# A transformer layer on one core: the last output projection but one asked for earlier, weight sums one group later, later loads tied

## The chip, the cores and the metric

One NeuronCore of a Trainium2 chip runs the whole program. The metric is the device time of one execution in microseconds (us), as a median of several runs. Engines are named as in the profile: PE (TensorE matmuls; PEld is its weight loads), DVE (VectorE), ACT (ScalarE), POOL (GpSimd), SP (SyncE, which here only issues DMAs).

## The reference, cut to what matters

One layer, 2048 tokens, width 1024, feed-forward width 4096, all float32:

```
h = rmsnorm(x, norm_mix) * (1 + sc_a) + sh_a
x = x + g_a * hybrid_mixer(h, ...)           # stick-breaking attention and gated delta rule, then @ w_out
h = rmsnorm(x, norm_mlp) * (1 + sc_m) + sh_m
x = x + g_m * (square(relu(h @ w_ff1)) @ w_ff2)
```

The change concerns the end of the mixer (`@ w_out`), the second norm and the feed-forward.

## The kernel before

**Precision.** A float32 product is made of three float32r matmuls: every operand is split into a rounded part and a rest (`hm`/`lm`, `who`/`wlo`, `bh`/`bl`, `swh`/`swl`), ACT makes the rounded part by a cast and DVE or POOL the rest by a subtraction.

**Mixer.** The tokens are four chunks of 512, worked from chunk 3 down to chunk 0. `project_out(c)` (L943 to L968) multiplies a chunk's mixed heads by `w_out`: it loads 8 tiles `mx`, splits them into `hm` and `lm` (L950, L132), makes 8 output tiles of 24 matmuls each (192 in all, L221 to L223), adds the residual (L959), stores the sum to `x1_d[c]`, and collects its squares. `outs(c)` calls it and asks for the norm's factors. Chunk 0's delta rule is a chain that goes from engine to engine in small steps (L901 to L939); a branch (L575) stands inside it, whose body is not entered here.

**Feed-forward.** It runs in two halves of 1024 tokens, `hf` 1 (chunks 2, 3) and then `hf` 0. Both products use a scheme of 7 block products in place of 8, which needs sums of blocks. The right sides of the first product, `bs` (28 split tiles), are made from `x1_d`: each tile is loaded, scaled twice (`load_x`, L1095), summed on POOL and split (`split_right`). For `hf` 1 that is written out at L1117 to L1129, for `hf` 0 in `load_h` (L1195 to L1227). `ff1` (L1249) runs 16 groups `g` of 7 products with 12 matmuls each (84 a group, L1260 to L1262); its left sides come from `lefts1` (four loads `A` of 256 KB, four POOL sums `s`, split by `left`, L1139). Its result goes to `h_d` in seven parts. `ff2` (L1307) runs 112 products of 12 matmuls (L1337 to L1339), each with a weight `w` and a right tile `bl` loaded and split; its sums `y` start from `x1_d` (`load_y`, L1228).

**The weight sums.** `w_ff2` has to be summed as well. `sums2(g)` (L1237) does it during `hf` 1: it loads 1 MB into two tiles `ws`, makes two sums on POOL (L1242, L1244) and two on DVE (L1243, L1245), and stores 1 MB to `w2_d[g]`. It is called ahead of `ff1(hf, g, ...)`.

**What sets the order.** A scheduler builds each engine's list of instructions before the run: it goes by the order of the program, with `tc.high_priority()` pulling work ahead and `tc.issue_after(x)` keeping an instruction behind `x`. On the chip every engine takes its list strictly in turn, so an instruction that waits holds up all behind it.

Of the kernel before, what the change touches and what calls it, by code (L numbers as in the profile page):

```python
# [7 lines left out]
F32 = mybir.dt.float32  # L8
# [49 lines left out]
def tile_hybrid_layer(  # L58
# [17 lines left out]
    nc = tc.nc  # L76
# [57 lines left out]
    if True:  # L134
# [17 lines left out]
        def full(tag, name, bufs=1, dt=F32, pool=None):  # L152
            return (pool or np_).tile([P, CH], dt, tag=tag, name=name, bufs=bufs)
# [46 lines left out]
        late = []  # L200

        def run_late():

            todo, late[:] = late[:], []
            for f in todo:
                f()
# [849 lines left out]
        def outs(*which):  # L1056
            for o_ in which:
                acc = project_out(o_)
                if o_:
                    out_rstd(o_, acc)  # L1060
                accs2[o_] = acc
# [33 lines left out]
        def load_x(hf, rs, x, k, i, n):  # L1095
            kk = k + 4 * i
            nc.sync.dma_start(x, x1_d[2 * hf + n][:, kk, :])
            V.tensor_tensor(x, x, rs[n], ALU.mult)
            A.activation(x, x, AF.Identity, scale=g2[:, kk:kk + 1], bias=mods[:, 24 + kk:25 + kk])
            return x  # L1100
# [5 lines left out]
        outs(2)  # L1106
        run_late()
        run_late()
        rs1 = [full("acc1", "frs2"), full("wab", "frs3", pool=k1)]
        for n in range(2):  # L1110
            nc.sync.dma_start(rs1[n], rs_d[2 + n])
# [4 lines left out]
        for k in range(4):  # L1116
# [10 lines left out]
            split_right(bs[5][k], x22)  # L1127
            G.tensor_tensor(x21, x22, x21, SUB)
            split_right(bs[3][k], x21)  # L1129
        outs(1, 0)  # L1130

        casts = []

        def left(x, name, eng):  # L1139

            wh = wp.tile([P, CH], F32R, tag="wh", name="swh" + name)
            wl = wp.tile([P, CH], F32R, tag="wl", name="swl" + name)
            with tc.high_priority():
                casts.append(A.copy(wh, x).ins)  # L1144
                eng.tensor_tensor(wl, x, wh.bitcast(F32), SUB)  # L1145
            return wh, wl

        def lefts1(hf, g, unit):

            nm = f"{hf}_{g}"  # L1150
            a = []
            with tc.high_priority():
                for i, t in enumerate(AB):
                    u = unit(t, f"{t}_1{nm}")
                    gate["w1"] = nc.sync.dma_start(u, w_ff1[g, i]).ins
                    a.append(u)
                a11, a12, a21, a22 = a
                s4, s5, s2, s6 = [unit("S", f"s{i}{nm}") for i in (4, 5, 2, 6)]
                G.tensor_tensor(s4, a21, a22, ADD)
                G.tensor_tensor(s5, s4, a11, SUB)  # L1160
                G.tensor_tensor(s2, a12, s5, SUB)
                G.tensor_tensor(s6, a11, a21, SUB)
            xs = (a11, a12, s2, a22, s4, s5, s6)
            return lambda j: left(xs[j], f"{nm}_{j}", V)

# [29 lines left out]
        def load_h(hf, rs):  # L1195
            bs = rights(hf)

            def load(tag, i, n):
                return [load_x(hf, rs, unit(tag, f"fx{hf}{k}{i}{n}"), k, i, n) for k in range(4)]

            def split(j, xs):
                for k in range(4):
                    split_right(bs[j][k], xs[k])

            def sub(o, x, y):
                for k in range(4):
                    G.tensor_tensor(o[k], x[k], y[k], SUB)

            x11, x12 = load("A11", 0, 0), load("A12", 0, 1)
            split(0, x11)  # L1210
            sub(x11, x12, x11)
            split(4, x11)
            x22 = load("A22", 1, 1)
            sub(x11, x22, x11)
            split(5, x11)
            split(2, x22)
            sub(x12, x22, x12)
            split(6, x12)
            x21 = load("A21", 1, 0)
            sub(x11, x11, x21)  # L1220
            split(3, x11)
            split(1, x21)
            return bs
# [11 lines left out]
        def sums2(g):  # L1235

            y = [fy.tile([P, N2], F32, tag="y", name=f"ws2_{g}_{i}") for i in range(3)]  # L1237
            (a11, a12), (a21, a22), (s4, s5) = [(t[:, 0:CH], t[:, CH:N2]) for t in y]
            for i in range(2):
                with tc.issue_after(gate["w1"]):  # L1240
                    nc.sync.dma_start(y[i].rearrange("p (i c) -> p i c", i=2), w_ff2[g, 2 * i:2 * i + 2].rearrange("i p c -> p i c"))
            G.tensor_tensor(s4, a21, a22, ADD)  # L1242
            V.tensor_tensor(s5, s4, a11, SUB)  # L1243
            G.tensor_tensor(a11, a11, a21, SUB)  # L1244
            V.tensor_tensor(a12, a12, s5, SUB)  # L1245
            for i in range(2):
                nc.sync.dma_start(w2_d[g][:, 2 * i:2 * i + 2], y[2 - 2 * i].rearrange("p (i c) -> p i c", i=2))

        def ff1(hf, g, bs, get):  # L1249
            nm = f"{hf}_{g}"  # L1250
# [56 lines left out]
        def ff2(hf, q, ys, base):  # L1307


            n1, n2 = 0, CH  # L1310
            dst = {0: ((0, n1),), 1: ((0, n1),), 5: ((0, n2),), 2: ((0, n2),), 4: ((4, n2),), 6: ((4, n1), (4, n2)),
                   3: ((4, n1),)}
            chain = {0: "u", 5: "u", 6: "u", 4: "v", 2: "v", 3: "p", 1: "q"}
            a, banks = q % 2, {}
            side = {"u": a, "v": 1 - a, "p": 1 - a, "q": a}
            final = {n: j for j in ORDER for n in dst[j]}
            for n, j in enumerate(ORDER):
                ch = chain[j]
                start = ch not in banks
                if start:  # L1320
                    banks[ch] = [pf.tile([P, CH], F32, tag=f"f{side[ch]}", name=f"f2{hf}_{q}_{j}{m}") for m in range(4)]
                for i in range(8):
                    g = 8 * q + i
                    nm = f"2{hf}_{g}_{j}"
                    x, bt = unit("S", "w" + nm), right_tile(nm)
                    nc.sync.dma_start(x, {0: w_ff2[g, 0], 1: w_ff2[g, 1], 3: w_ff2[g, 3]}[j] if j in (0, 1, 3) else
                                      w2_d[g][:, {4: 0, 5: 1, 6: 2, 2: 3}[j], :])
                    nc.sync.dma_start(bt[1].bitcast(F32), h_d[hf][g][:, j, :])
                    at = 56 * q + 8 * n + i
                    with tc.issue_after(casts[base + max(at - 22, at // 4 - 3)]):  # L1330
                        A.copy(bt[0], bt[1].bitcast(F32))  # L1331
                    V.tensor_tensor(bt[1], bt[1].bitcast(F32), bt[0].bitcast(F32), SUB)  # L1332
                    wh, wl = left(x, nm, G)
                    for m in range(4):
                        s = slice(m * P, (m + 1) * P)
                        ps = banks[ch][m]
                        T.matmul(ps, lhsT=wh[:, s], rhs=bt[0], start=start and i == 0, stop=False, skip_group_check=True)  # L1337
                        T.matmul(ps, lhsT=wh[:, s], rhs=bt[1], start=False, stop=False, skip_group_check=True)  # L1338
                        T.matmul(ps, lhsT=wl[:, s], rhs=bt[0], start=False, stop=i == 7, skip_group_check=True)  # L1339
                with tc.high_priority():  # L1340
                    for m in range(4):
                        for m0, cs in dst[j]:
                            y = ys[m0 + m][:, cs:cs + CH]
                            gt = ngate[:, m0 + m:m0 + m + 1] if j == 3 else mods[:, 40 + m0 + m:41 + m0 + m]
                            V.scalar_tensor_tensor(y, banks[ch][m], gt, y, ALU.mult, ALU.add)  # L1345
                            if q == 1 and final[m0, cs] == j:
                                nc.sync.dma_start(yTv[:, m0 + m, hf * N2 + cs:hf * N2 + cs + CH], y)
# [3 lines left out]
        def get(j):  # L1351
            return first.get(j) or rest(j)

        for hf in (1, 0):
            if not hf:
                get = lefts1(0, 0, unit)
            for g in range(NG):
                more = lefts1(hf, g + 1, unit) if g + 1 < NG else None
                if hf:
                    sums2(g)  # L1360
                ff1(hf, g, bs, get)
                get = more
                if hf and g == 1:
                    for f in rstd([accs2[0]], "2", "20", pf, "f0"):
                        f()
                if not hf and g == 4:
                    ys = load_y(0)
            if hf:
                ys = load_y(1)
            base = len(casts)  # L1370
            for q in range(2):
                ff2(hf, q, ys, base)
            if hf:
                bs = load_h(0, [accs2[0], accs2[1]])
# [88 lines left out]
```

## Time and profile before

| | us |
|---|---|
| median of 3 runs (lowest, highest) | 2860.49 (2858.39, 2870.82) |
| the profiled execution | 2859.91 |
| its span, first to last instruction | 2858.1 |
| PE busy in the span | 2579.9 |
| DVE, ACT, POOL busy | 1651.4, 1286.4, 1041.4 |

PE has the most busy time, so PE's idle time and the time that it spends at its lower clock are what a change can win back. The profile's column PEclk gives the granted clock as a share of the full 2.4 GHz; half of it is 1.2 GHz. Stages are best read one by one, since each has another limit.

### The profile page before, as it was taken

To read this page: it belongs to the slowest core of one execution; us is meant where nothing else is said; L and a number is where in the kernel's file an instruction comes from. 1 tells how busy PE (TensorE), PEld (TensorE's weight loads), DVE (VectorE), ACT (ScalarE), POOL (GpSimd) and SP (SyncE) were. 2 spreads that over 40 slices of the span, in tenths; PEclk is the share of its full clock that TensorE was granted. 3 is DMA by queue.
4 is the path that set the end of the run, shared out by engine and by line. 5 is a ranking of instruction groups with operands and counts; after the bars stand their busy time and mean duration, and the time that the engine had idled before them with its cause. 6 is when DMAs were issued, how large, how long until landed. Compare 5 with 4: busy or idle time off the path is not lost. (4 is left out here: it accounts for less than half of the span.)

```text
span 2858.1 us, 40676 instructions
## 1 busy us (share of the span) xinstructions
PE 2579.9 (90%) x13684; PEld 2105.0 (74%) x13684; DVE 1651.4 (58%) x3359; ACT 1286.4 (45%) x2622; POOL 1041.4 (36%) x837
## 2 busy tenths in 40 slices
PE   4998789899999999899288988889999999999999
PEld 2787568877787787777167777767887888878887
DVE  7653886377445774257554655576556544476551
ACT  4552453245334454245343444455443555564441
POOL 3222200040012201021235666654447555655444
PEclk9999889999999999899599999999999999999999
DMA  9786687574556556453265666696664464476664
GB/s 305 271 293 209 201 281 255 161 226 156 175 172 199 186 172 208 132 170 117 64 191 193 214 210 214 217 364 217 194 192 148 138 212 151 155 263 197 194 186 130
DMA packets 327314, 566.85 MB, mean 198 GB/s; under 512 B 33512, under 2 KB 80552, under 8 KB 327080
## 3 DMA queue, kind: packets, MB, share of 16 engines
q1 hardware_dynamic: 308904, 534.63, 57.2%
q10 hardware_dynamic: 18176, 29.37, 2.8%
q8 instruction: 114, 1.87, 0.3%
q14 instruction: 120, 0.98, 0.1%
HBM read 403.86 MB, written 160.01 MB: 197 GB/s over the span
## 5 line engine op out<-in xcount | busy, mean ns | idle before, releaser
L1145 POOL TENSOR_TENSOR swl<-w,swh 128x512 fp32r<-128x512 f32 x224 | 301.1, 1346 | 310.0 <-ACT swh L1144 300.0
L1262 PE MATMUL f<-bh,swl 128*128 128x512 f32 x896 | 353.5, 400 | 33.2 <-DVE swl L1145 33.2
L1260 PE MATMUL f<-bh,swh 128*128 128x512 f32 x896 | 358.3, 400 | 11.4 <-ACT swh L1144 8.8
L1337 PE MATMUL f<-bh,swh 128*128 128x512 f32 x896 | 352.0, 393 | 13.3 <-ACT swh L1144 13.3
L1261 PE MATMUL f<-bl,swh 128*128 128x512 f32 x896 | 355.8, 397 | 0.0
L1332 DVE TENSOR_TENSOR bl<-bl,bh 128x512 fp32r<-128x512 f32 x224 | 263.8, 1194 | 159.0 <-ACT bh L1331 158.8
L1338 PE MATMUL f<-bl,swh 128*128 128x512 f32 x896 | 351.5, 392 | 0.0
L1339 PE MATMUL f<-bh,swl 128*128 128x512 f32 x896 | 335.4, 392 | 7.7 <-POOL swl L1145 7.7
L1144 ACT CAST swh<-w 128x512 fp32r<-128x512 f32 x224 | 139.1, 621 | 331.7 <-POOL swl L1145 256.9
L1262 PEld LDWEIGHTS f<-bh,swl 128*128 128x128 f32 x896 | 172.5, 193 | 75.8 <-DVE swl L1145 39.1
L1260 PEld LDWEIGHTS f<-bh,swh 128*128 128x128 f32 x896 | 173.1, 193 | 51.1 <-ACT swh L1144 9.7
L1337 PEld LDWEIGHTS f<-bh,swh 128*128 128x128 f32 x896 | 169.8, 189 | 50.4 <-ACT swh L1144 15.0
L1339 PEld LDWEIGHTS f<-bh,swl 128*128 128x128 f32 x896 | 169.5, 190 | 45.1 <-POOL swl L1145 9.8
L1261 PEld LDWEIGHTS f<-bl,swh 128*128 128x128 f32 x896 | 173.1, 193 | 36.6 <-issue 0.2
L1338 PEld LDWEIGHTS f<-bl,swh 128*128 128x128 f32 x896 | 169.9, 190 | 35.6
L1145 DVE TENSOR_TENSOR swl<-s,swh 128x512 fp32r<-128x512 f32 x126 | 141.4, 1127 | 83.5 <-ACT swh L1144 83.2
L221 PE MATMUL mmo<-hm,who 128*128 128x512 f32 x256 | 102.1, 405 | 45.8 <-ACT hm L950 45.7
L1145 DVE TENSOR_TENSOR swl<-A,swh 128x512 fp32r<-128x512 f32 x95 | 88.4, 930 | 87.2 <-ACT swh L1144 87.2
L1274 ACT ACTIVATE t<-t 128x512 f32<-128x512 f32 x128 | 80.6, 630 | 126.9 <-DVE t L1273 126.9
L1331 ACT CAST bh<-bl 128x512 fp32r<-128x512 f32 x224 | 135.2, 615 | 2.2 <-DMA bl<-h_d 2.2
L932 POOL TENSOR_TENSOR o<-o,ro 128x512 f32<-128x512 f32 x16 | 16.6, 1040 | 320.4 <-DVE ro L129 158.3
L1273 DVE TENSOR_TENSOR t<-t,f 128x512 f32<-128x512 f32 x128 | 87.2, 683 | 68.7 <-PE f L1262 65.6
(380 smaller groups left out, 6094.2 us busy)
## 6 DMA issues: line engine op xcount, KB each, us to landing
bl<-h_d SPq DMA_DIRECT2D x224, 256.0 KB
A<-in_w_ff_dram SPq DMA_DIRECT2D x128, 256.0 KB
h_d<-t SPq DMA_DIRECT2D x128, 256.0 KB
w<-w_d SPq DMA_DIRECT2D x128, 256.0 KB
wada<-in_w_ada_dram SPq DMA_DIRECT2D x48, 512.0 KB
h_d<-T SPq DMA_DIRECT2D x96, 256.0 KB
w<-in_w_ff_dram SPq DMA_DIRECT2D x96, 256.0 KB
wso<-in_w_out_dram SPq DMA_DIRECT2D x64, 256.0 KB
```

The source lines that it names most:

```text
L221: T.matmul(ps, lhsT=wh[:, k % 4, :], rhs=ah, start=k == 0, stop=False)
L1144: casts.append(A.copy(wh, x).ins)
L1145: eng.tensor_tensor(wl, x, wh.bitcast(F32), SUB)
L1260: T.matmul(ps, lhsT=wh[:, s], rhs=ah, start=start and k == 0, stop=False, skip_group_check=True)
L1261: T.matmul(ps, lhsT=wh[:, s], rhs=al, start=False, stop=False, skip_group_check=True)
L1262: T.matmul(ps, lhsT=wl[:, s], rhs=ah, start=False, stop=stop and k == 3, skip_group_check=True)
L1273: V.tensor_tensor(t, t, ps, op)
L1331: A.copy(bt[0], bt[1].bitcast(F32))
L1332: V.tensor_tensor(bt[1], bt[1].bitcast(F32), bt[0].bitcast(F32), SUB)
L1337: T.matmul(ps, lhsT=wh[:, s], rhs=bt[0], start=start and i == 0, stop=False, skip_group_check=True)
L1338: T.matmul(ps, lhsT=wh[:, s], rhs=bt[1], start=False, stop=False, skip_group_check=True)
L1339: T.matmul(ps, lhsT=wl[:, s], rhs=bt[0], start=False, stop=i == 7, skip_group_check=True)
```

## The change

Three things are altered, and the matmuls, sums and bytes stay as they are.

1. `outs(1)`, the output projection of the last chunk but one, is asked for in front of the block that makes the right sides of `hf` 1; only `outs(0)` stays behind it.
2. `sums2(g)` now issues its loads and returns a function `make` with the four sums and the stores. The main loop calls it one group later, and ties the sums to that group's left sides (`gate["left"]`, `lows[-1]`).
3. In `load_h` the loads of `hf` 0's right sides are tied to the issue of certain late `bl` loads of `ff2`, and its splits, one by one, to casts of `ff2`.

```diff
         outs(2)
         run_late()
         run_late()
+        outs(1)
         rs1 = [full("acc1", "frs2"), full("wab", "frs3", pool=k1)]
...
-        outs(1, 0)
+        outs(0)
...
-                eng.tensor_tensor(wl, x, wh.bitcast(F32), SUB)
+                low = eng.tensor_tensor(wl, x, wh.bitcast(F32), SUB).ins
+                if eng is V:
+                    lows.append(low)
...
-                G.tensor_tensor(s6, a11, a21, SUB)
+                gate["left"] = G.tensor_tensor(s6, a11, a21, SUB).ins
...
         def load_h(hf, rs):
             bs = rights(hf)
+            at = [len(casts) - 28]
             def load(tag, i, n):
-                return [load_x(hf, rs, unit(tag, f"fx{hf}{k}{i}{n}"), k, i, n) for k in range(4)]
+                with tc.issue_after(gate["h"][at[0] - len(casts) - 12]), tc.issue_after(casts[at[0]]):
+                    return [load_x(hf, rs, unit(tag, f"fx{hf}{k}{i}{n}"), k, i, n) for k in range(4)]
             def split(j, xs):
                 for k in range(4):
-                    split_right(bs[j][k], xs[k])
+                    with tc.issue_after(casts[min(at[0] + 4, len(casts) - 1)]):
+                        split_right(bs[j][k], xs[k])
+                    at[0] += 1
...
-            G.tensor_tensor(s4, a21, a22, ADD)
-            V.tensor_tensor(s5, s4, a11, SUB)
-            G.tensor_tensor(a11, a11, a21, SUB)
-            V.tensor_tensor(a12, a12, s5, SUB)
-            for i in range(2):
-                nc.sync.dma_start(w2_d[g][:, 2 * i:2 * i + 2], y[2 - 2 * i].rearrange("p (i c) -> p i c", i=2))
+            def make():
+                with tc.issue_after(gate["left"]), tc.issue_after(lows[-1]):
+                    G.tensor_tensor(s4, a21, a22, ADD)
+                    V.tensor_tensor(s5, s4, a11, SUB)
+                    G.tensor_tensor(a11, a11, a21, SUB)
+                    V.tensor_tensor(a12, a12, s5, SUB)
+                for i in range(2):
+                    nc.sync.dma_start(w2_d[g][:, 2 * i:2 * i + 2], y[2 - 2 * i].rearrange("p (i c) -> p i c", i=2))
+            return make
...
                 if hf:
-                    sums2(g)
+                    late.append(sums2(g))
+                if len(late) > 1 or late and not more:
+                    late.pop(0)()
                 ff1(hf, g, bs, get)
...
+            for f in late:
+                f()
+            late = []
             if hf:
                 ys = load_y(1)
```

How the lists of instructions move, at three places.

PE, behind the branch in chunk 0's delta rule (`p` and `pot` are that chain, `mmo` an output projection). Before:

```order
L575 UNCONDITIONAL_BRANCH x2
L901 MATMUL p_0_101_19795<-S_0_111_19788,wq_0_1_19686 128x128 x2
L911 MATMUL p_0_100_19792<-vz_224,ktok_0_0_19396 128x128 x2
L914 MATMUL p_0_100_19792<-vz_224,AT_0_0_19633 128x128 x2
L911 MATMUL p_0_101_19795<-vz_224,ktok_0_0_19396 128x128 x2
L914 MATMUL p_0_101_19795<-vz_224,AT_0_0_19633 128x128 x2
L935 MATMUL pot_0_1_19835<-cst,o_0_1_19767 128x128 x4
```

After, from the 22nd matmul behind the branch on:

```order
L222 MATMUL mmo_0_3_27459<-lm_0_27282,who_0_30_27461 128x512
L901 MATMUL p_0_101_19795<-S_0_111_19788,wq_0_1_19686 128x128 x2
L911 MATMUL p_0_100_19792<-vz_224,ktok_0_0_19396 128x128 x2
L914 MATMUL p_0_100_19792<-vz_224,AT_0_0_19633 128x128 x2
L223 MATMUL mmo_0_3_27459<-hm_0_27281,wlo_0_30_27462 128x512
L221 MATMUL mmo_0_3_27459<-hm_1_27287,who_0_30_27461 128x512
```

The projection of chunk 1 now stands between the steps of the chain: 52 of its 192 matmuls ahead of the branch, 140 behind it, and all of these ahead of the chain's last L901 (`p_0_001`). The splits of the right sides (L132 on DVE, L1092 on ACT) still follow the chain's last L939, and chunk 0's `hm` still follows the last of their loads' scalings.

DVE, the weight sums of `hf` 1 (`ws_3` is group 3's). Before, group 3's sums stand ahead of group 3's first left side, `swl_3_0`:

```order
L1145 TENSOR_TENSOR swl_2_3_28898<-A_11_2_28576,swh_2_3_28897 128x512
L1273 TENSOR_TENSOR t_2_1_28802<-t_2_1_28802,f_2_4_28827 128x512
L1145 TENSOR_TENSOR swl_2_1_28918<-A_11_2_28572,swh_2_1_28917 128x512
L1243 TENSOR_TENSOR ws_3_2_28969<-ws_3_2_28969,ws_3_0_28967 128x512
L1245 TENSOR_TENSOR ws_3_0_28967<-ws_3_0_28967,ws_3_2_28969 128x512
L1145 TENSOR_TENSOR swl_3_0_28983<-A_11_3_28774,swh_3_0_28982 128x512
```

After, group 2's sums stand there, behind six of group 3's seven left sides:

```order
L1146 TENSOR_TENSOR swl_3_6_29049<-s_3_28779,swh_3_6_29048 128x512
L1146 TENSOR_TENSOR swl_3_3_29069<-A_11_3_28774,swh_3_3_29068 128x512
L1254 TENSOR_TENSOR ws_2_2_28786<-ws_2_2_28786,ws_2_0_28784 128x512
L1285 TENSOR_TENSOR t_3_1_28973<-t_3_1_28973,f_3_4_28998 128x512
L1256 TENSOR_TENSOR ws_2_0_28784<-ws_2_0_28784,ws_2_2_28786 128x512
```

Group 3's own sums stand at the same place in group 4, behind `swl_4_3`. The loads of `ws` have kept their distance from the loads `A`.

SP, the start of `ff2` in `hf` 1 (`w`, `bl` are what `ff2` needs, `fx` the loads for `hf` 0's right sides). Before:

```order
L1097 DMA fx_34004<-x_d_112 128x512
L1294 DMA h_d_15_28332<-t_15_3_31089 128x512
L1326 DMA w_5_0_31379<-in_w_ff_dram 128x512
L1328 DMA bl_2_2_31880<-h_d_2_28319 128x512
L1328 DMA bl_3_2_31903<-h_d_3_28320 128x512
L1294 DMA h_d_15_28332<-t_15_2_31088 128x512
L1097 DMA fx_34008<-x_d_112 128x512
L1326 DMA w_6_0_31402<-in_w_ff_dram 128x512
```

After, at the same distance from the start of the list:

```order
L1340 DMA bl_0_2_31834<-h_d_0_28317 128x512
L1338 DMA w_7_0_31425<-in_w_ff_dram 128x512
L1340 DMA bl_1_2_31857<-h_d_1_28318 128x512
L1340 DMA bl_2_2_31880<-h_d_2_28319 128x512
L1306 DMA h_d_15_28332<-t_15_1_31081 128x512
L1340 DMA bl_3_2_31903<-h_d_3_28320 128x512
L1340 DMA bl_4_2_31926<-h_d_4_28321 128x512
L1306 DMA h_d_15_28332<-T_15_1_31217 128x512
L1239 DMA y_6_31254<-x_d_114 128x512
```

All 16 `fx` loads have left this place; the first stands a hundred places further on, behind `bl_8_5`. The last three of the eight `y` tiles have come in here, behind the last weight sums.

## Rows read from the trace of the kernel before

**Rows 1.** The page, part 1: busy time, share of the span, instructions.

```profile
PE 2579.9 (90%) x13684; PEld 2105.0 (74%) x13684; DVE 1651.4 (58%) x3359; ACT 1286.4 (45%) x2622; POOL 1041.4 (36%) x837
```

**Rows 2.** Windows, stage by stage: length; busy PE, PEld, DVE, ACT, POOL; PEclk, DMA share, GB/s.

```profile
1356.90:1390.30 33.40, 15.56 (x80) 14.06 (x80) 17.82 (x59) 3.99 (x6) 2.08 (x2) 0.66 0.12 34
1390.30:1431.20 40.90, 0.00 (x0) 0.00 (x0) 26.48 (x33) 20.73 (x34) 18.20 (x14) 0.50 0.32 90
1431.20:1482.70 51.50, 48.26 (x192) 37.12 (x193) 26.82 (x33) 22.46 (x38) 21.92 (x16) 0.92 0.64 198
1482.70:1538.20 55.50, 46.68 (x203) 36.90 (x202) 19.90 (x38) 17.93 (x31) 18.96 (x15) 0.97 0.51 165
1538.20:1908.00 369.80, 332.28 (x1354) 266.19 (x1355) 208.45 (x230) 177.07 (x311) 228.75 (x159) 0.94 0.67 234
1908.00:2239.80 331.80, 313.53 (x1345) 256.67 (x1344) 210.23 (x210) 150.89 (x263) 180.31 (x133) 0.97 0.62 198
```

**Rows 3.** Timeline, end of the mixer: start, length, instruction, [idle before, releaser].

```profile
1361.64 1.19 PE L901 MATMUL p<-S,wq 128*128 128x128 f32 x4 [4.01 <-PEq L575]
...
1379.59 0.68 PE L901 MATMUL p<-S,wq 128*128 128x128 f32 x4 [0.56 <-DVE o L922]
...
1389.55 0.75 DVE L939 SCALAR_TENSOR_TENSOR sz<-pot,vecs,sz 128x512 f32<-128x512 f32 x1 [2.42 <-PE pot L935]
...
1431.23 1.22 PE L221 MATMUL mmo<-hm,who 128*128 128x512 f32 x2 [41.72 <-ACT hm L950]
...
1538.24 0.80 PE L1260 MATMUL f<-bh,swh 128*128 128x512 f32 x1 [6.46 <-ACT swh L1144]
```

**Rows 4.** Timeline, one weight sum in the first product of half 1.

```profile
1598.29 1.02 SPq L1241 DMA_DIRECT2D ws<-in_w_ff_dram  x2
...
1606.81 1.26 POOL L1242 TENSOR_TENSOR ws<-ws 128x512 f32<-128x512 f32 x1 [4.75 <-DMA ws<-in_w_ff_dram]
1608.10 0.69 DVE L1243 TENSOR_TENSOR ws<-ws,ws 128x512 f32<-128x512 f32 x1 [7.20 <-POOL ws L1242]
...
1611.24 0.80 PE L1262 MATMUL f<-bh,swl 128*128 128x512 f32 x1 [4.18 <-DVE swl L1145]
```

**Rows 5.** Waits in 1538 to 1908: us in total, times, longest.

```profile
POOL ws L1242 <- DMA ws<-in_w_ff_dram: 79.0, 13, 7.7
...
PE f L1262 <- DVE swl L1145: 33.2, 14, 4.2
```

**Rows 6.** Windows, single groups of both products.

```profile
1538.20:1564.20 26.00, 23.20 (x87) 18.31 (x88) 15.87 (x13) 8.26 (x14) 17.52 (x13) 0.87 0.63 228
...
1586.20:1606.40 20.20, 19.76 (x86) 15.87 (x85) 12.01 (x11) 10.16 (x19) 13.11 (x9) 1.00 0.65 233
1606.40:1632.60 26.20, 22.02 (x86) 17.62 (x86) 13.17 (x15) 12.37 (x22) 15.14 (x11) 0.87 0.62 202
...
2258.90:2277.90 19.00, 19.00 (x85) 15.76 (x84) 9.36 (x11) 11.03 (x19) 11.00 (x9) 1.00 0.45 152
1908.00:1946.70 38.70, 25.14 (x98) 19.00 (x96) 35.03 (x41) 24.44 (x44) 15.29 (x11) 0.88 0.96 360
...
2166.50:2196.30 29.80, 25.09 (x97) 19.82 (x96) 14.82 (x13) 9.67 (x17) 29.06 (x20) 0.89 0.31 97
```

**Rows 7.** DMA issues in 1885 to 1950, one line of the list.

```profile
fx<-x_d SPq DMA_DIRECT2D x16, 256.0 KB
```

**Rows 8.** Timeline, late in the second product of half 1.

```profile
2168.75 6.85 POOL L1207 TENSOR_TENSOR fx<-fx,fx 128x512 f32<-128x512 f32 x4
...
2184.39 2.07 PE L1339 MATMUL f<-bh,swl 128*128 128x512 f32 x4 [4.04 <-POOL swl L1145]
```

**Rows 9.** Timeline, POOL and DVE at work at the same time.

```profile
1597.36 1.74 POOL L1161 TENSOR_TENSOR s<-A,s 128x512 f32<-128x512 f32 x1
...
1599.16 1.74 DVE L1145 TENSOR_TENSOR swl<-A,swh 128x512 fp32r<-128x512 f32 x1
```

**Rows 10.** Windows, the stretch ahead of the branch, columns as in the stages.

```profile
1251.90:1356.90 105.00, 97.79 (x674) 76.10 (x672) 77.83 (x194) 56.17 (x152) 26.38 (x25) 0.95 0.45 147
```

More of the change, by code (lines that the diff above doesn't have):

```diff
@@ L1129, in tile_hybrid_layer @@
             split_right(bs[3][k], x21)
-        outs(1, 0)
-        casts = []
+        outs(0)
+        casts, lows = [], []
         def left(x, name, eng):
@@ L1327, in ff2 @@
                                       w2_d[g][:, {4: 0, 5: 1, 6: 2, 2: 3}[j], :])
-                    nc.sync.dma_start(bt[1].bitcast(F32), h_d[hf][g][:, j, :])
+                    gate["h"].append(nc.sync.dma_start(bt[1].bitcast(F32), h_d[hf][g][:, j, :]).ins)
                     at = 56 * q + 8 * n + i
@@ L1352, in get @@
             return first.get(j) or rest(j)
+        late, gate["h"] = [], []
         for hf in (1, 0):
```

## The prediction

> **What bounds the kernel now.** I read four views in this order: the page's busy times, the windows by stage, then the timeline and the waits inside each stage that is longer than its matmuls. PE is busy 90% of the span [rows 1], so it is the engine whose idle time counts. The windows show where the other 10% lies [rows 2]. In half 0 a group of the first product takes 19.0 us with PE never idle and the full clock granted [rows 6], so 16 would take 304; in half 1 they take 369.8, 66 us more, at a mean granted clock of 0.94. The second product of half 1 takes 331.8. And from 1356.9 to 1431.2 PE does only 15.6 us of work in 74.3.
>
> Inside these stages:
>
> - At 1431.2 PE has waited 41.7 us for `hm`, the cast of the mixed heads [rows 3]. The chain of the delta rule ended at 1390.3 (1389.55 + 0.75), and between the two ACT, DVE and POOL make the right sides of half 1. Both last projections are queued behind that.
> - In the first product the loads of the weight sums are issued at 1598.3; POOL starts the sum at 1606.8, DVE's own sum has then waited 7.2 us at the head of DVE's queue, and PE misses a left side for 4.2 us [rows 4]. POOL waited 79.0 us for such loads in the stage, in 13 places, and PE 33.2 us for the left sides [rows 5]. The rest of the 66 us is the clock, which falls to half after such a gap: it averages 0.87 in the group of 26.2 us in which that gap lies, and 1.00 in one of 20.2 [rows 6].
> - The second product's first eight products take 38.7 us, where 8 x 12 matmuls at 19.0 / 84 us would take 21.7 [rows 6]. DMA is 96% busy there, and 16 loads for the *next* half's right sides are among its transfers [rows 7]. Late in it a group takes 29.8 us: four sums of right sides stand in one piece of 6.85 us on POOL, ahead of left sides, and PE waits 4.0 us [rows 8].
>
> **Term 1, the projection.** A matmul costs 19.0 / 84 = 0.226 us at the full clock [rows 6], so the projection's 192 cost 43.4 us wherever they stand. *What goes.* Now the first projection behind the right sides takes 51.5 us, with a slow start, and the second 55.5 up to the first product's begin [rows 2]. With one left it pays the slow start of the first, and then the 6.5 us in which PE waits for the first left side of the feed-forward [rows 3]. So 107.0 becomes 58.0, and 49.0 us leave. The wait of 41.7 us stays: the lists still put the right sides between the chain's end and `hm`. *What comes.* 52 matmuls (11.8 us) stand ahead of the branch, where PE has 7.2 us idle in 105 [rows 10]; DVE gets 8 splits and 4 weight rests there, 12 x 0.69 = 8.3 us at the length of DVE's row at 1608.1 [rows 4], on an engine busy 76 of 105. Between 4.6 (all idle time filled) and 16; I take 13, since PE was full there and the chain also waits for DVE. 140 matmuls (31.7 us) stand behind the branch, among the chain. Now 17.95 us pass from 1361.64 to the chain's last L901 at 1379.59 [rows 3]. Then PE must do 31.7 and the chain's own matmuls ahead of that point, about 7 us at the full clock (15.56 us for 80 at a mean clock of 0.66 [rows 2], of which some 55 lie here): 38.7, so the chain ends 20.8 later, between 15 and 25. Gain 49.0 - 13 - 20.8 = **15** (8 to 29). The projection's DMAs stand on SP between those of the chain, as the second projection's stand now; weights are asked for more than 24 matmuls (5.4 us) ahead of their use in the new list, so I cost them at nothing; if that cover is gone, PE stands with the chain behind it, which is the lower end. The right sides start later by the 33.8 us that the chain is late, and stay next: they are what PE waits for.
>
> **Term 2, the weight sums.** Their bytes, and two instructions on each engine per group, stay. The sums now meet loads issued more than a group (19 us) ahead, where 8.5 us passed from issue to use [rows 4]. So POOL's 79.0 us of waiting, DVE's behind it and PE's 33.2 go, with the half clock. What is late next is the first group: 26.0 us against 19.0 [rows 6], which waits for its own loads; it keeps its 7. Floor: 16 x 19.0 + 7 = 311. POOL has ten instructions a group; at 1.26 alone and up to 1.74 beside DVE [rows 4, 9] that is 13 to 17 us of 19, so now and then a left side will be late; I add 5 for it. 369.8 - 316 = **54**. Ends: 66 (304, all groups at 19.0) and 40 (every group at 20.2, the fastest with sums that the rows show, plus 7).
>
> The row at 1599.2 shows a DVE subtraction of 1.74 us beside POOL's sums, where 0.69 is its length with POOL at rest [rows 4, 9]. The Trainium skill, "SBUF — State Buffer", section "SBUF: two separate sides", says why: an instruction of VectorE with two SBUF inputs and one of GpSimd lock a shared pair of ports against each other, for the whole instruction. By that, ten POOL and nine such DVE instructions need 10 x 1.26 + 9 x 0.69 = 18.8 us of the pair per group, just under PE's 19.0, and the trace agrees as far as the lengths go. Moving the sums does not lighten that load, which speaks against the change, and it is the first rival below.
>
> **Term 3, the tied loads.** Of the 17.0 us that the first eight products lose, the 16 loads (4.2 MB of the 13.9 MB that 360 GB/s move in 38.7 us) go, but three of eight `y` tiles (1.5 MB) come in, behind the last weight sums: I take 11. The sums of right sides now stand as two, one, one, five and, much later, four between left sides, where it was four, four, one: from the first to the last of the run 13 POOL instructions against four products, 17 to 20 us against 10.9, about 8 late where it was about 10. So of the 8.1 us lost at 2166 some 3 go. Together **14**, between 0 and 22 (17 + 5).
>
> **Sum.** 15 + 54 + 14 = 83; 2859.9 - 83 = 2777 us for the execution profiled, which lies 0.6 under the median of the three runs. With the ends, 2743 to 2812. Half a per cent, 14 us, is about what a measurement of this kernel can tell from no change.
>
> **Rivals.**
>
> - *The port pair or POOL bounds the first product.* For it: the groups without a gap still took 20.2 and not 19.0 [rows 6]. Against it: PE was busy 19.8 of these 20.2. All groups at 20.2 and the first's 7: 330, so term 2 is 40, and 2791.
> - *DMA bounds it.* A group moves four loads of 256 KB, seven stores of 256 KB and 2 MB for the sums: 4.98 MB, 262 GB/s at 19 us, where the stage moved 234 [rows 2]. At 234 a group takes 21.3: 348 with the first's 7, term 2 is 22, term 3 falls to 4: 2819. Against it: 360 GB/s at 96% in the next stage [rows 6], and 234 at a share of 0.67.
> - *The projection brings nothing*, since the chain is delayed by as much as leaves: 2792. For it: 43.4 us of matmuls are filled into 17.8 + 7.2 us of idle time, so most is only moved. Against it: the slow starts are paid once, not twice.
> - *Slower: the sums hold up DVE in every group.* POOL's first sum now stands behind the last sum of the next group's left sides, which waits for DVE's sixth split, and DVE's sum stands two instructions later. If POOL comes more than two products (5.4 us) late there, DVE stands, the seventh left side and the next group's are late, and each group costs what the worst one does, 26.2 [rows 6]: 419, 49 more than now; with 15 + 14 of the other terms, 2880. Against it: POOL is ahead of that point by the loads' waits that vanish.
> - *The ties change only the list and the chip runs as before*: 2858 to 2862. The rows of the lists speak against it.
>
> **How the numbers follow.** My forecast 0.60 (2743 to 2812 is its own range), port pair 0.14, projection worth nothing 0.10, DMA 0.09, slower 0.04, no effect 0.03. The first four are all under 2846, faster by over half a per cent: 0.93; same 0.03; slower 0.04. The range takes in the first four: 2745 to 2822.
>
> **What would show it.** Right: PE's wait for `hm` is still 38 to 45 us, but only 192 projection matmuls follow it, and some 140 stand among the chain; POOL's waits for `ws` loads fall from 79 to under 5; the first product of half 1 takes 311 to 325 us at a clock of 0.98 or more; the second product's first eight take under 32. Wrong: the wait for `hm` longer by over 10 us, or the chain's end over 45 us later than now (term 1); a first product above 335 with PE waiting for `swl` (port pair, POOL) or for DMA; the start of the second product no shorter, with PE behind loads of `w`.

## The result and the profile after

The changed kernel takes 2824.89 us (median of 4 runs, 2824.29 to 2830.35); the kernel before took 2859.44 beside it. The ratio is 0.9875, 95% interval 0.9847 to 0.9904: 35 us faster, where 83 were forecast (2777, range 2745 to 2822). The direction held; more than half of the gain is missing, and the time lies 3 us above the range.

The page, part 1 of the changed kernel, to be read against [rows 1]: the same work, in a span 35.0 us shorter.

```profile
PE 2576.0 (91%) x13684; PEld 2104.8 (75%) x13684; DVE 1641.1 (58%) x3359; ACT 1285.2 (46%) x2622; POOL 1040.0 (37%) x837
```

Windows by stage (columns as in [rows 2]): the chain with the projection between its steps, the wait for `hm` with the second part of the chain, the last projection, the first and the second product of half 1. (From 1464.2 on the edges lie 0.3 to 0.4 us late; the lengths of both products are right.)

```profile
1354.00:1388.20 34.20, 32.80 (x184) 27.38 (x183) 14.80 (x33) 12.83 (x25) 7.66 (x6) 1.00 0.39 125
1388.20:1464.20 76.00, 28.93 (x152) 24.49 (x152) 47.75 (x89) 30.81 (x51) 30.64 (x24) 0.70 0.40 125
1464.20:1526.00 61.80, 51.87 (x203) 40.58 (x203) 27.48 (x47) 21.70 (x37) 21.66 (x17) 0.86 0.44 145
1526.00:1877.40 351.40, 322.38 (x1356) 260.04 (x1356) 193.96 (x225) 170.02 (x304) 221.05 (x158) 0.97 0.66 230
1877.40:2204.50 327.10, 311.06 (x1346) 255.78 (x1345) 214.06 (x217) 155.11 (x270) 186.60 (x134) 0.98 0.67 218
```

The first product's first matmul stands at 1525.6, 12.6 earlier than before. The product takes 351.4 where it took 369.8, 18.4 less, and the second 327.1 for 331.8, 4.7 less. Together 35.7; half 0 takes 0.7 more, so this is the whole gain. The projection brought 12.6 of its 15, the weight sums 18 of 54, the ties 5 of 14. These lengths are of one profiled execution each (e7 below shows how far one can be off).

**The end of the mixer** went as forecast. From the timeline, PE's first matmul behind the branch, DVE's last step of the chain, the first matmul behind `hm` and the first of the first product:

```profile
1375.43 0.47 PE L222 MATMUL mmo<-lm,who 128*128 128x512 f32 x1 [1.41 <-PEq L575]
...
1423.01 0.75 DVE L939 SCALAR_TENSOR_TENSOR sz<-pot,vecs,sz 128x512 f32<-128x512 f32 x1 [2.39 <-PE pot L935]
...
1463.88 0.79 PE L221 MATMUL mmo<-hm,who 128*128 128x512 f32 x1 [40.91 <-ACT hm L950]
...
1525.63 0.79 PE L1272 MATMUL f<-bh,swh 128*128 128x512 f32 x1 [6.67 <-ACT swh L1145]
```

The chain ends at 1423.8, 33.5 later than at [rows 3] (33.8 forecast): 13.8 of it up to PE's first matmul behind the branch (13 forecast) and 19.7 from there on (20.8). PE still waits 40.9 for `hm`, and one projection stands behind it.

**The first product.** Its waits (us in total, times, longest), to be read against [rows 5]:

```profile
POOL s L1162 <- DMA A<-in_w_ff_dram: 94.1, 13, 8.6
...
DVE ws L1254 <- POOL ws L1253: 57.8, 13, 6.2
...
PE f L1274 <- DVE swl L1146: 26.9, 14, 3.3
```

POOL's 79.0 us for the loads of the weight sums are gone, as the prediction wanted. But POOL now waits 94.1 us in 13 places for the loads `A` of the left sides, and PE still waits in 14 places for a rest `swl`, 26.9 us where it was 33.2. One turn of this, in the timeline of SP, POOL, DVE and PE:

```profile
1650.23 1.09 SPq L1249 DMA_DIRECT2D ws<-in_w_ff_dram  x2
1653.19 0.34 SPq L1258 DMA_DIRECT2D w_d<-ws  x1
...
1655.16 0.32 SPq L1258 DMA_DIRECT2D w_d<-ws  x1
1655.53 0.99 SPq L1158 DMA_DIRECT2D A<-in_w_ff_dram  x1
...
1663.12 1.29 POOL L1162 TENSOR_TENSOR s<-A,A 128x512 f32<-128x512 f32 x1 [8.58 <-DMA A<-in_w_ff_dram]
...
1672.77 1.29 POOL L1253 TENSOR_TENSOR ws<-ws 128x512 f32<-128x512 f32 x1
...
1674.09 1.76 DVE L1254 TENSOR_TENSOR ws<-ws,ws 128x512 f32<-128x512 f32 x1 [6.17 <-POOL ws L1253]
...
1677.82 0.32 SPq L1258 DMA_DIRECT2D w_d<-ws  x1
1678.19 0.89 SPq L1158 DMA_DIRECT2D A<-in_w_ff_dram  x1
1678.40 0.79 PE L1274 MATMUL f<-bh,swl 128*128 128x512 f32 x1 [3.30 <-DVE swl L1146]
```

In the kernel before, the load went out ahead of the stores in most groups, 7.7 us ahead in this one:

```profile
1577.64 1.06 SPq L1241 DMA_DIRECT2D ws<-in_w_ff_dram  x2
...
1579.25 0.43 SPq L1155 DMA_DIRECT2D A<-in_w_ff_dram  x1
1586.90 0.33 SPq L1247 DMA_DIRECT2D w_d<-ws  x1
```

The changed kernel has a ring here. POOL's first left sum (L1162) needs the load of `A21`, the last of a group's four loads in SP's list. That load is issued at 1655.5, right behind the stores of the weight sums of an earlier group, and behind 1 MB of `ws` loads; POOL's sum starts 7.6 us later. POOL's left sums are then late, its weight sum L1253 stands behind them in its list, DVE stands 6.2 us at its own weight sum L1254 and makes the next rests late; the stores wait for DVE, and the next `A21` (1678.2) waits behind the stores.

**The second product.** Windows of single groups (before: [rows 6]): its first eight products, and the eight with the sums of right sides between them. Then PE's two longest waits in the first stretch, from the timeline, each with the cast on ACT that it waits for.

```profile
1877.40:1913.40 36.00, 24.18 (x97) 18.89 (x96) 30.48 (x33) 22.97 (x41) 17.51 (x13) 0.91 1.04 398
2133.10:2161.00 27.90, 23.68 (x98) 19.15 (x97) 12.92 (x13) 10.73 (x19) 27.86 (x20) 0.94 0.34 103
```

```profile
1891.75 0.62 ACT L1145 CAST swh<-w 128x512 fp32r<-128x512 f32 x1 [3.17 <-DMA w<-in_w_ff_dram]
1892.42 0.50 PE L1349 MATMUL f<-bh,swh 128*128 128x512 f32 x1 [4.36 <-ACT swh L1145]
...
1912.32 0.62 ACT L1145 CAST swh<-w 128x512 fp32r<-128x512 f32 x1 [2.68 <-DMA w<-w_d]
1912.99 0.79 PE L1349 MATMUL f<-bh,swh 128*128 128x512 f32 x1 [6.68 <-ACT swh L1145]
```

The 16 `fx` loads have left the first stretch [rows 7], and it still takes 36.0 us, with DMA at a share of 1.04 and PE behind loads of `w`.

### The profile page after: what moved, and what is told of

Read it like the earlier page. It is cut to its first block, busy times and chain, and to the rows that moved or that the text cites. A ratio compares the mean times of both kernels' runs of the same rounds, so it can differ in the third digit from the quotient of the medians.

```text
span 2823.1 us, 40704 instructions
## 1 busy us (share of the span) xinstructions
PE 2576.0 (91%) x13684; PEld 2104.8 (75%) x13684; DVE 1641.1 (58%) x3359; ACT 1285.2 (46%) x2622; POOL 1040.0 (37%) x837
## 5 line engine op out<-in xcount | busy, mean ns | idle before, releaser
L1274 PE MATMUL f<-bh,swl 128*128 128x512 f32 x896 | 349.7, 396 | 26.9 <-DVE swl L1146 26.9
L1274 PEld LDWEIGHTS f<-bh,swl 128*128 128x128 f32 x896 | 170.7, 191 | 69.1 <-DVE swl L1146 33.2
L1146 DVE TENSOR_TENSOR swl<-s,swh 128x512 fp32r<-128x512 f32 x126 | 127.9, 1017 | 119.4 <-ACT swh L1145 119.0
L1343 ACT CAST bh<-bl 128x512 fp32r<-128x512 f32 x224 | 136.2, 615 | 12.6 <-DMA bl<-h_d 12.4
L496 POOL TENSOR_TENSOR akf<-akf,rkb 128x640 f32<-128x640 f32 (+1 forms) x16 | 25.3, 1578 | 260.1 <-issue 72.5
```

Source lines behind the costliest of these rows:

```text
L1146: low = eng.tensor_tensor(wl, x, wh.bitcast(F32), SUB).ins
L1274: T.matmul(ps, lhsT=wl[:, s], rhs=ah, start=False, stop=stop and k == 3, skip_group_check=True)
```

## The experiments

Three theories for the first product. ORDER: `A21` goes out late, since SP's list has it behind stores that wait for sums. BYTES: it lands late, since 2 MB lie ahead of it or beside it. PORT: POOL and DVE hinder each other, whatever SP does. The totals are medians, the three columns of stages are from the one profiled execution of each kernel; the kernel before took 2860.5 to 2863.2 beside the runs. "Group" is the mean of the 3rd to the 15th group of the first product in half 1, from the starts of their first matmuls; "eight" the second product's first eight products.

| run | us | ratio (95%) | first product | group | eight |
|---|---|---|---|---|---|
| before | 2860 | | 369.8 | 23.3 | 38.7 |
| changed | 2824.9 | 0.9875 (0.9847 to 0.9904) | 351.4 | 22.0 | 36.0 |
| e1 projection alone | 2845.2 | 0.9946 (0.9928 to 0.9964) | 366.7 | 23.1 | 39.4 |
| e5 sums alone | 2843.4 | 0.9929 (0.9913 to 0.9946) | 350.6 | 21.9 | 40.0 |
| e9 ties alone | 2840.5 | 0.9933 (0.9914 to 0.9953) | 368.8 | 23.2 | 22.7 |
| e2 | 2802.5 | 0.9791 (0.9773 to 0.9810) | 331.9 | 20.5 | 35.7 |
| e3 | 2800.2 | 0.9776 (0.9752 to 0.9801) | 326.3 | 20.1 | 35.4 |
| e4 | 2803.8 | 0.9797 (0.9779 to 0.9815) | 332.6 | 20.5 | 35.6 |
| e6 | 2909.4 | 1.0166 (1.0149 to 1.0183) | 351.3 | 22.0 | 22.6 |
| e7 | 2813.7 | 0.9832 (0.9794 to 0.9871) | 358.6 | 22.5 | 26.4 |
| e8 | 2884.7 | 1.0074 (1.0047 to 1.0101) | 331.1 | 20.1 | 21.8 |
| e10 | 2787.4 | 0.9755 (0.9730 to 0.9781) | 329.9 | 20.1 | 25.1 |
| e11 | 2783.6 | 0.9743 (0.9717 to 0.9768) | 330.9 | 20.1 | 23.7 |
| e12 no sums | 2771.5 | 0.9693 (0.9665 to 0.9722) | 312.9 | 19.1 | 25.3 |
| e13 | 2770.6 | 0.9670 (0.9642 to 0.9697) | 321.4 | 19.1 | 23.4 |
| e14 | 2769.7 | 0.9674 (0.9647 to 0.9701) | 314.2 | 19.1 | 25.6 |

### The three parts, each alone

e1 has only the moved `outs(1)`, e5 only the weight sums one group later, e9 only the tied `load_h`, each put into the kernel before, with the lines of the change's diff.

> The kernel before with the last but one output projection asked for ahead of the first right sides, and nothing else. The changed kernel's profile has the first product start 12.2 us earlier (1526.0 against 1538.2). If that is this part's whole worth: about 2847, ratio 0.9957 (0.994 to 0.997). If the part and the sums help each other (the first product's loads and weight sums meet a queue that the tail has cleared), it is worth less alone: 2852 or more. If the cost of the tail is hidden in the old first product's stalls: none, 2857 to 2861.

> The kernel before with only the weight sums put one group behind their loads. In the changed kernel's profile the first product took 351.4 us (369.8 before), 18.4 less. If the part is worth that by itself: 2860 - 18 = 2842 (2837 to 2847), POOL's wait for the weight loads gone and its wait for A loads at the first left sum 80 us or more. If the other parts took something from it (the second theory: the tail or the tied loads crowd the queue): nearer to the forecast's 54, 2806 to 2825.

> The kernel before with only the later loads tied (the fx loads, their splits). The changed kernel's second product of the first half took 327.1 us against 331.8. If that is the ties' worth: 2860 - 5 = 2855 (2851 to 2859). If the ties work but the result loads that e7 moved take their gain at the start: the same, with the first eight products at 36 to 40 us and the gain of 2 us in the late group. If they are worth what was forecast: 2846.

Gains of 15.3, 19.2 and 20.9 us: 55 added up, 35 together. e1 and e5 are worth alone about what their stage shows in the changed kernel. e9 is not, and that was not expected: alone the ties win 16 us at the first eight products, where the change wins 2.7. The window of e9, and the issue of the loads into `y` in e9 and in the changed kernel (one line of each: durations, first and last start):

```profile
1907.60:1930.30 22.70, 22.40 (x98) 17.91 (x97) 22.66 (x19) 18.34 (x35) 18.27 (x12) 1.00 1.03 393
```

```profile
L1236 SPq DMA_DIRECT2D y<-x_d x16: 320/459/953, 1869.4 to 1886.3; - x16
```

```profile
L1239 SPq DMA_DIRECT2D y<-x_d x16: 319/378/1130, 1855.5 to 1906.5; - x16
```

In e9 the last of the 16 loads goes out 21 us ahead of the first product's end. In the changed kernel six of them go out behind it, after the stores of the last group's sums at 1880.9 and 1882.9: the weight sums, one group later, hold the tiles that `y` needs for longer (both come from the pool `fy` of 8). e5, which has the later sums alone, shows the same six loads behind the end of its first product, and e7 below takes the `y` loads away. What one part cleared, another filled.

Of the other two parts: in all thirteen profiles with the moved projection the first product starts between 1513.6 and 1527.5, in the three without it between 1538.2 and 1541.3. In e5 POOL waits 76.4 us for `A` loads at its first left sum (80 or more were expected).

### The load of `A21`

e2 emits a group's two stores one group later, behind `A21`'s load; e3 ties the two `ws` loads behind it as well; e4 does only that, and leaves the stores ahead.

```diff
-                    gate["w1"] = nc.sync.dma_start(u, w_ff1[g, i]).ins
+                    gate[i] = gate["w1"] = nc.sync.dma_start(u, w_ff1[g, i]).ins
...
-                with tc.issue_after(gate["w1"]):        # ws loads: e3, e4
+                with tc.issue_after(gate[2]):
...
+            def store():                                # called one group later: e2, e3
                 for i in range(2):
+                    with tc.issue_after(gate[2]):
                         nc.sync.dma_start(w2_d[g][:, 2 * i:2 * i + 2], y[2 - 2 * i].rearrange("p (i c) -> p i c", i=2))
```

> The changed kernel with the two stores of a group's weight sums emitted one group later and tied behind the load of A21 of the group after next to come, so that SP issues this load without waiting for the sums; the sums stay where they are. Theory ORDER (A21's load, which the first left-side sum on POOL reads, stands on SP's queue behind stores that wait for DVE's and POOL's weight sums: 94 us of POOL's wait): the load goes out about 4 us earlier in each group, POOL's wait for A loads at its first left sum falls from 94 to under 50, PE's waits for lows from 27 to under 10, the first product falls from 351 to 315 to 332 us, total 2790 to 2807. Theory BYTES (the load is late because 2 MB of weight loads and stores are moved ahead of it or beside it): the load still lands 7 us after its issue, behind the 1 MB of weight loads ahead of it; first product 343 to 351, total 2817 to 2825. Theory PORT (POOL and DVE are held up by each other's reads, whatever the queue does): no change, 2822 to 2827.

> As e2, and the two loads of the weights to be summed (1 MB) are tied behind A21's load as well. ORDER: within 4 us of e2, since the issue of A21 is freed in both. BYTES: the 1 MB no longer lies ahead of A21, which lands 3 to 4 us after its issue: clearly faster than e2, first product 315 to 330, total 2790 to 2805. PORT: no change, 2822 to 2827.

> The changed kernel with only the two loads of the weights to be summed tied behind A21's load, which still stands behind the stores. ORDER: A21 goes out when it did, the first product stays at 351 within 4, total 2821 to 2829. BYTES: 1 MB less ahead of A21, half or more of what the stall costs is won, first product 330 to 342, total 2803 to 2816. PORT: no change, 2822 to 2827.

All three win 21 to 25 us. The totals and first products of e2 came as ORDER said, those of e4 as BYTES said, and e3, with both, is no better than either by more than 4 us; PORT alone falls. One sign of ORDER missed: PE's waits for the rests fell to 15.2 us in e2, not under 10. So the load was late by both, and either repair opens the ring: what the second would give finds POOL waiting for something else. POOL's waits in e3, from 1526 to 1850:

```profile
POOL s L1162 <- DVE swl L1146: 58.8, 14, 4.4
...
POOL s L1162 <- DMA A<-in_w_ff_dram: 6.9, 1, 6.9
```

The 94.1 us of waiting for `A` have shrunk to one place; POOL now waits mostly for DVE's `swl`, which read the tiles of its earlier sums, and it can afford that: PE's wait for `swl` is 9.8 us there, and a group 19.94 in most places. Bandwidth was not short: from 1590 to 1850 e3 moved 258 GB/s at a share of 0.75, the changed kernel 225 at 0.65.

```profile
1590.00:1850.00 260.00, 251.09 (x1089) 203.32 (x1090) 151.47 (x172) 137.71 (x248) 179.72 (x128) 1.00 0.75 258
```

### The start of the second product

e6 ties each `bl` load behind the `w` load of the product five ahead, in place of up to 28; e7 takes the 16 `y` loads out of the beginning and puts each quarter among the eight products whose end first needs it; e8 is e3 with both.

```diff
+                    with tc.issue_after(ws_[max(len(ws_) - 6, 0)]):       # e6, e8; ws_: the w loads so far
                         gate["h"].append(nc.sync.dma_start(bt[1].bitcast(F32), h_d[hf][g][:, j, :]).ins)
...
+                    for m, c in [(m, c) for a_, c, m in gate["y"][hf].pop((q, n, i), [])]:     # e7, e8
+                        with tc.issue_after(ws_[-1]): nc.sync.dma_start(ys[m][:, c:c + CH], x1_d[2 * hf + c // CH][:, m, :])
```

> The changed kernel with each load of a right side of the second product (bl) tied on SP's queue behind the weight load of the product five ahead of its own, where up to 28 now go out ahead. Theory AHEAD (the first eight products wait because 36 such loads, 9 MB, of which they need 8, lie in front of their own loads): first eight from 36.0 to 26 to 30 us in the first half, and from 26.3 to 22 to 25 in the second, total 2810 to 2819. Theory RESULTS (the 4 MB of the x_d loads into y are what crowds it): 1 to 3 us, total 2820 to 2826. Theory OWN (the last group's own products and their stores come too late): none. Against: fewer loads ahead leave less cover later in the product, and the total may rise above 2825.

> The changed kernel with the sixteen loads into y for the first second product moved out of its beginning, each quarter in front of the eight products whose end first needs it. AHEAD: 4 MB less of some 24 in the stretch, 2 to 6 us, total 2818 to 2823. RESULTS: first eight from 36.0 to 25 to 29, total 2813 to 2818. OWN: none, 2822 to 2827.

> The kernel of e3 with both of these ties. AHEAD or RESULTS: e3's 2800 less the gains of e6 and e7, 2784 to 2792. OWN: as e3, 2797 to 2803.

The first eight products take 22.6, 26.4 and 21.8 us for 36.0. e6 does more there than AHEAD said (26 to 30), e7 what RESULTS said (25 to 29), and each does more than the other theory allowed it. So both kinds of load stand in the way, and OWN falls. The share of DMA is still 1.03 and 1.04 in these windows of e6 and e7: what counts in this stretch is what stands ahead of the loads that PE waits for. e7's total gains about as much as its window, though its runs spread widely (2804 to 2827). Its first product took 358.6 us, 7 more than the changed kernel's, with the same order of issues on SP up to 1855 us: by so much a single profile of that stage can be off. e6 and e8, though, lose some 85 us against the changed kernel and e3. ACT's waits in e6's second product of half 1:

```profile
ACT bh L1343 <- DMA bl<-h_d: 181.6, 91, 4.1
```

ACT's list still had the casts of these tiles up to 22 products ahead, and the loads now came 5 ahead, so ACT stood in line in 91 places, with the casts of the weights behind. The case against, named in the expectation, came true, and dearer than thought; the totals that AHEAD and RESULTS gave for e6 and e8 failed by it.

### Both repairs together

e10 is e3 with e7's tie alone. e11 adds a softer tie of the `bl` loads of products 8 to 39, with ACT's casts retied to match:

```diff
+                    with tc.issue_after(ws_[max(at // 2 - 4, 0) - at - 1]) if 8 <= at < 40 else nullcontext():
                         gate["h"].append(...)
-                    with tc.issue_after(casts[base + max(at - 22, at // 4 - 3)]):
+                    with tc.issue_after(casts[base + max(at - 22, at // 2 - 5)]):
```

> The kernel of e3 with only the ties of e7 (the loads into y), the right loads going out as in the changed kernel. If the two gains add: e3's 2800 less e7's 9.6 us at the first eight products, 2786 to 2793, first product 322 to 328, first eight 25 to 28. If the right loads take the y loads' place in the queue now that the first product ends earlier: 2794 to 2800.

> As e10, with the right loads of products 8 to 39 tied behind the weight load of half their number less four, and their casts on ACT tied alike (cast number half less five), so that ACT's list no longer asks for what the queue holds back, which is what the 178 us of ACT's wait for these loads in e6 say happened. If this is the cause of e6's loss: first eight 22 to 25 in both halves, no loss later, total 2779 to 2787. If the second product needs the long lead for itself (transfers that come late under load, whatever ACT's order): a loss of 20 or more as in e6, 2805 to 2880.

e10's total is where it was expected, 2787.4: the two repairs add. (Its first product missed the 322 to 328; the last group takes 24.5 us, where e3's takes 20.5.) e11 has no loss later. It differs from e6 in two things, ACT's list and a lead of 8 to 24 products in place of 5, so it shows that the loads can be paced without the loss, and not which of the two cures it; that e6's loss came from the list rests on ACT's 181.6 us. In half 0 its first eight products take 21.9 us where e10's take 26.0. Its total is 4 us lower, which the overlapping intervals do not settle.

### What is left in a group

A group with sums still took 19.94 us, without them 19.04 (half 0). e12 is e10 without the sums: the 32 on POOL and 32 on DVE are left out, and the stores hold loaded weights. e13 and e14 are e11 with all four sums of a group on POOL, or on DVE.

```diff
                 with tc.issue_after(gate["left"]), tc.issue_after(lows[-1]):      # e12: all four lines out
                     G.tensor_tensor(s4, a21, a22, ADD)      # e14: V
-                    V.tensor_tensor(s5, s4, a11, SUB)
+                    G.tensor_tensor(s5, s4, a11, SUB)       # e13
                     G.tensor_tensor(a11, a11, a21, SUB)     # e14: V
-                    V.tensor_tensor(a12, a12, s5, SUB)
+                    G.tensor_tensor(a12, a12, s5, SUB)      # e13
```

> As e10, without the weight sums themselves: the 32 sums on POOL and 32 on DVE are left out, their loads and stores stay (the stores hold the loaded weights instead). Theory PORT for what is left (a group of 19.94 us in e3 against 19.0 in the second half, which has no sums): group 19.0 to 19.2, first product 308 to 314, total 10 to 15 below e10. If the loads and stores are what is left: group 19.7 to 20, total within 4 of e10.

> The kernel of e11 with the two weight sums of DVE moved to POOL, so that DVE no longer stands in line for POOL's first one. Theory LINE (DVE's in-order wait of 3.7 us a group makes the first product's lows late): group from 19.94 to 19.0 to 19.2, total 10 to 14 below e11, 2769 to 2775. Theory PORT (work of the sums on either engine slows the other): POOL's 10 operations of 1.3 to 1.75 us become 12, about 17.5 us of 19; group 19.6 to 20.5, total within 6 of e11 or above.

> The kernel of e11 with the two weight sums of POOL moved to DVE. LINE: no wait for POOL, but four sums of 0.7 to 1.7 us in DVE's list ahead of lows: group 19.0 to 19.6, total 5 to 14 below e11. PORT: POOL has less, DVE more; group 19.4 to 20.

Without the sums 0.9 us a group go, 16 us in all, which is what PORT said, but which LINE would give as well. e13 and e14 tell them apart: with the sums, but none of them waiting for the other engine, the same 0.9 go, as LINE said and PORT did not. In e10 DVE stands once a group at its first sum (the line names the load that came last; the sum L1253 on POOL ends as DVE starts):

```profile
1637.99 1.27 POOL L1253 TENSOR_TENSOR ws<-ws 128x512 f32<-128x512 f32 x1
...
1639.30 1.76 DVE L1254 TENSOR_TENSOR ws<-ws,ws 128x512 f32<-128x512 f32 x1 [3.67 <-DMA A<-in_w_ff_dram]
```

and a group of e13 has PE never idle, with twelve instructions on POOL:

```profile
1649.00:1668.00 19.00, 19.00 (x85) 15.72 (x85) 10.20 (x12) 11.00 (x20) 16.88 (x12) 1.00 0.77 264
```

The port pair does not bound this product. By the sum that the prediction made of the Trainium skill's page "SBUF — State Buffer", section "SBUF: two separate sides", e13 would need an estimated 12 x 1.26 + 7 x 0.69 = 19.95 us of the pair in each group; it takes 19.0, so here the measurement decides against that sum. It does not decide against the waiting itself. Three rows of the same group:

```profile
1655.61 1.30 POOL L1313 TENSOR_TENSOR t<-t,t 128x512 f32<-128x512 f32 x1
...
1655.62 1.84 DVE L1146 TENSOR_TENSOR swl<-s,swh 128x512 fp32r<-128x512 f32 x1 [1.39 <-ACT swh L1145]
1656.85 1.75 POOL L1315 TENSOR_TENSOR T<-t,T 128x512 f32<-128x512 f32 x1
```

The rest that starts with POOL's sum ends 0.55 us behind that sum's end, and the next POOL sum 1.14 us behind the rest's end. From 1593 to 1800 all 64 rests over 0.8 us in e13 end 0.55 or 0.56 us behind a POOL row, and all 44 POOL rows over 1.45 us end 1.15 or 1.16 us behind a DVE row: the two take turns. So a row's length is more than its turn takes, which is why the sum came out too high, and PE does not wait for these rests.

e13 and e14 are 3.3% faster than the kernel before and 1.9% faster than the changed one by their medians, the best of this study.

## Why the prediction was right and wrong

**Term 1, the projection: right.** 12.6 us of 15, in its range, and by its own steps: the chain 33.5 us later (33.8 forecast, and both of its parts within 1.1), the wait for `hm` 40.9 (38 to 45), one projection behind it. What is missing lies in that last projection, 61.8 us up to the first product where 58.0 were taken. e1 shows the term alone: 15.3.

**Term 2, the weight sums: right in its mechanism, wrong in what comes next.** The wait that it was to remove went: POOL waits for the sums' loads no more. The step that failed reads "What is late next is the first group". What was late next was the load of `A21` in every group, at 94.1 us in 13 places. Two things had been left out. The change moved the stores of the sums, on SP's queue, to a place ahead of that load (1579.3 ahead of 1586.9 before, 1655.5 behind 1655.2 after), and I followed the sums through POOL and DVE but not the stores through SP. And I held the `ws` loads to be harmless once they are early, though their 1 MB lies ahead of the 256 KB that POOL needs first. That cost 21 to 25 us of the 36 missing (e2 to e4). The price of POOL's sum for DVE is about 13 groups of 0.9, 12 us (e13, e14), in place of the 5 that I added for a late left side.

**Term 3, the ties: worth more than forecast, and eaten.** Alone they win 20.9 us, 16 of them at the first eight products (e9). The step that failed is the 11 us taken for "three of eight `y` tiles (1.5 MB) come in". The size was right (six loads, 1.5 MB), the price was not: they and the last stores are issued in the stretch itself, in front of the loads that PE waits for, while the 36 `bl` loads were not counted at all. In this full queue what counted was what stood ahead, and not the bytes of the whole stretch: e9, e7 and e6 take 22.7, 26.4 and 22.6 us at a share of 1.03 or 1.04. The late group gained 1.9 for the 3 taken.

**The rivals.** *DMA bounds it* gave 348 us for the first product, 4 for term 3 and 2819, all within a few us of what came. That was luck, since its mechanism was wrong: it had the bandwidth at its limit at 234 GB/s, and e3 and e13 move 258 and 264 in the same product. The rate that looked like a limit came from the waits in a ring. *The port pair* falls with e13 and e14, as a bound of this product. *Slower* had a true mechanism, DVE in line behind POOL's first sum, in every group and 57.8 us in all; but it priced every group at 26.2 us, where they take 22.0, and without the late `A21` it costs 0.9. *Projection worth nothing* and *no effect* fall with e1, e5 and e9.

**The signs named ahead** worked: a first product above 335 us with PE waiting for `swl`, and a start of the second product that is hardly shorter, with PE behind loads of `w`, were both listed as wrong, and both were seen. The first sign was put down to the port pair or POOL's load, though, and the cause was another.

## What to carry to other kernels

When work is moved behind its loads, follow its stores through the issuing queue too: a store stands there until its sum is done, and any load behind it inherits that wait. When a wait is removed, ask for each in-order list in the ring which load it needs first, and put that load ahead of the large ones that can come later. Price parts of a change that share a queue or a pool of tiles together, since here 15, 19 and 21 us made 35.

## What was not expected of the hardware

DMA moved up to 407 GB/s in 1877 to 1895 of the changed kernel at a share of 1.05, so the 360 GB/s at 0.96 from which term 3 took its time were not the full rate. And a lead of five products in place of up to 28 cost 85 us in e6 without any more bytes: in half 1 alone ACT stood 182 us in its list for loads that each came at most 4.1 us late.
